# A pool at the far end of SBUF for the expert combination's factors and residuals, and an earlier overflow condition

## The chip, the cores and the metric

The kernel runs on one core of a Trainium2 chip. A core has five engines with a queue of instructions each: TensorE (PE in the profile; PEld is its loading of weights), VectorE (DVE), ScalarE (ACT), GpSimd (POOL) and SyncE (SP), which here mostly starts transfers; sixteen DMA engines carry them. The metric is the device time of one execution in microseconds, 4062.14 us before the change (median of three runs, 4050.82 to 4066.87).

## The reference, cut to what matters

Two blocks of a transformer run one behind the other over 2048 tokens of width 1024. The first ends in a mixture of experts with two experts for a token; the second begins with a norm and one wide projection:

```
# end of the first block
y = hierarchical_moe(h, ...)             # sum over the token's 2 experts: weight * expert's row
x = x + ga2 * rmsnorm(y, ln2_post)       # factor row: ga2 * ln2_post
# begin of the second block
h = rms_norm(x, gain2)
proj = h @ w_in_2                        # split into the inputs of two kinds of attention
```

The experts are a gate, an up and a down product of 1024 x 256, `silu(gate) * up` between them. All products are made in single precision as sums over high and low halves of the operands.

## The kernel before

**Who sets the order.** The program is written out once, in Python. Coroutines (lanes) yield until a model clock (`Clock`, line 35) thinks their operands ready; `B.run` then takes the next, and the order in which operations are written down is each engine's order. A change of what is ready when, or of where a transfer stands, can thus move the order of everything that is planned behind it. Each operation is issued by one helper, so nearly all rows of the profile show line 122, and the tile's name tells which operation it is.

**The experts** (`MoE`, line 1514). Tokens are sorted into 48 tiles of 128 rows: 32 experts and `NBIG` = 16 further tiles for experts with over 128 tokens. A tile's rows are gathered by an indirect DMA of GpSimd (`xg`) and transposed (`xh`). An expert's weights come as six loads of 512 KB (`ld`, four of gate and up, `in_w_gu`, two of down, `in_w_dn`). Each is split into a high half (`whi`, ScalarE) and a low half (`wlo`, VectorE). Then follow the two products (`pA`, and `pU` into `ym`), and a store of `ym` to the tile's rows of `Y` in HBM. The loop of `run` (from line 1656) starts with each tile's first product and ends with the product down of the tile before.

**The overflow** (`Overflow`, line 1689). If an expert had more tokens than its tiles take, a general program would do the whole layer again. Seven small VectorE operations on the counts (`ovm`, `ovj`, `ovn`) make a number `ovi` behind the last tile. `values_load` (line 1710) has every engine load it into a register, and each branches on it at line 1711. With these inputs the general program is skipped.

**The combination** (`Combine`, line 1807) is a lane of the second block's first stage, `S3.run`. `setup` loads the factor row `crow`, spread to all partitions; a load of `gain`, the second block's gain, follows. For each of sixteen blocks of 128 tokens, `block` gathers the two expert rows (`cy0`, `cy1` in the text of the code; the trace calls all of them `cy`) by indirect DMA and loads the residual `cx`. `finish` scales the first (ScalarE), adds the second (VectorE), squares for the norm (ScalarE), multiplies by norm and `crow` (VectorE), adds the residual (GpSimd), stores `X2`, and hands `cx` to the norm of the second block, which squares it again (`jk`), multiplies by `gain` (VectorE) and gives it to TensorE for transposing.

**The weights of the projection** (`Weights`, line 398) have one load buffer here (`b.nld = 1`), and are split like the experts': `whi` on ScalarE, `wlo` on VectorE; the third to sixth go to spare tiles of the combination's pool, `whix` and `wlox`. A load waits for the split of the one before. Eight of the sixteen blocks pass at the start of the stage, the others some 190 us later.

**Pools.** A pool takes its place in SBUF when it is opened and gives it back when it is closed. The combination's pool (`s_c`, in `S3.run`) is opened behind the condition. `crow`, `gain` and `cx` lie in it, so their loads stand behind the branch in SP's queue.

Of the kernel before, what the change touches and what calls it, by code (L numbers as in the profile page):

```python
# [22 lines left out]
T = 2048  # L23
# [184 lines left out]
class B:  # L208
# [15 lines left out]
        nc.vector.memset(self.eps, EPS)  # L224

    @contextmanager
    def pool(self, name):
        with self.tc.tile_pool(name=name, bufs=2, reuse_waits="tile") as p:
            yield Pool(p, self.clock)

    def phase(self, name):
# [1282 lines left out]
class MoE:  # L1514

    def __init__(self, b, H2, Y):
        self.b, self.nc, self.I, self.H2, self.Y = b, b.nc, b.I, H2, Y

        self.at = [t // 3 * 2 + t % 3 // 2 for t in range(NE + NBIG)]
        self.NT = len(self.at)
# [121 lines left out]
    def run(self):  # L1644
        st, en = self.b.phase("mo")
        with st:
            self.setup(en)
            W, NT = self.W, self.NT
            for t in range(4):
                self.gather(t)  # L1650
            W.split(3)
            for _ in self.xT(self.xg[0]):
                pass
            prev = None
            for t in range(NT + 1):
                cur = None
                if t < NT:
                    cur = (self.x, self.at[t])
                    g = self.gu(*cur)
                    next(g), next(g)  # L1660
                if prev:
                    a = self.aT(prev[0])

                W.split(5 + 4 * t + 2)
                if cur:
                    for _ in g:
                        pass
                    s = self.act(self.g)
                xt = self.xT(self.xg[(t + 1) % 4]) if t + 1 < NT else iter(())
                dn = self.down(a, *prev[1:]) if prev else iter(())  # L1670
                for i in range(2):
                    next(dn, None)
                    next(xt, None)
                    if i:
                        next(dn, None)
                for _ in xt:
                    pass
                W.split(5 + 4 * t + 4)
                if t == 2:
                    self.positions()  # L1680
                if t < NT:
                    self.gather(t + 4)
                    prev = (s, cur[1], t)
# [5 lines left out]
class Overflow:  # L1689


    def __init__(self, b, H2, Y, X2, big=NBIG):
        self.b, self.nc, self.I, self.H2, self.Y, self.X2, self.big = b, b.nc, b.I, H2, Y, X2, big

    def run(self):
        b, nc, tc = self.b, self.nc, self.b.tc
        st, en = b.phase("ov")
        with st:

            mx = b.small([128, 1], "ovm")  # L1700
            mi = b.small([128, 1], "ovi", I32)
            nc.vector.tensor_reduce(mx, b.cnt, axis=AX.X, op=OP.max)

            nb, jk = b.small([128, 1], "ovn"), b.small([128, NE], "ovj")
            nc.vector.tensor_scalar(jk, b.cnt, 128.0, None, op0=OP.is_gt, op1=OP.add, accum_out=nb)
            nc.vector.tensor_scalar(nb, nb, float(self.big), None, op0=OP.subtract)
            nc.vector.scalar_tensor_tensor(mx, mx, 256.0, nb, op0=OP.subtract, op1=OP.max)
            nc.vector.tensor_scalar(mx, mx, 0.0, None, op0=OP.max)
            nc.vector.tensor_copy(mi, mx)
            v = nc.values_load(mi[0:1, 0:1], min_val=0, max_val=T)  # L1710
            with tc.If(v > 0):
                with self.b.pool("ov_p") as P:
                    self.general(P)

    def general(self, P):
        b, nc, tc, I = self.b, self.nc, self.b.tc, self.I
# [90 lines left out]
class Combine:  # L1807


    def __init__(self, b, Y, X1, X2, ROW):  # L1810
        self.b, self.nc, self.Y, self.X1, self.X2, self.ROW = b, b.nc, Y, X1, X2, ROW
        self.started = False

    def setup(self, P):
        self.P = P
        self.row = P.tile([128, D], F32, name="crow", bufs=1)
        self.nc.sync.dma_start(self.row, bass.AP(tensor=self.ROW.tensor, offset=self.ROW.offset + 3 * D, ap=[[0, 128], [1, D]]))

    def block(self, blk, then=None):

        b, nc, P = self.b, self.nc, self.P
        ys = []
        for k in range(2):
            y = yield from P.get([128, D], F32, f"cy{k}", bufs=3)
            yield from b.G("indirect_dma_start", out=y, out_offset=None, in_=self.Y,
                           in_offset=bass.IndirectOffsetOnAxis(ap=b.pos[:, k, blk:blk + 1].bitcast(U32), axis=0),
                           bounds_check=self.Y.shape[0] - 1, oob_is_err=False)
            ys.append(y)
        x = yield from P.get([128, D], F32, "cx", bufs=4)
        yield from b.load(x, self.X1[blk * 128:blk * 128 + 128, :])  # L1830
        b.spawn(self.finish(blk, x, *ys, then))

    def finish(self, blk, x, y1, y2, then):
# [24 lines left out]
class S3:  # L1858
# [982 lines left out]
    def run(self):  # L2841
        b, tc, nc, I = self.b, self.b.tc, self.nc, self.I
        unit = [I["w2n"][g, i].rearrange("p k n -> p (k n)") for g in range(6) for i in range(2)]
        unit += [I["w2t"][j].rearrange("p k n -> p (k n)") for j in range(32)]
        unit += self.tail_units()

        order = []
        for u in range(44):
            order.append(u)
            if u - 20 in self.with_tail:  # L2850
                order.append(44 + self.with_tail.index(u - 20))
        self.at = {(0, u): n for n, u in enumerate(order)}
        self.at.update({(1, u): len(order) + u for u in range(44)})
        srcs = [unit[u] for u in order] + list(range(44))
        self.iw = b.const.tile([128, NTB, 8], F32, name="iw")
        self.bad = b.const.tile([128, NTB], F32, name="bad")
        nc.vector.memset(self.bad, 0.0)
        st0, en0 = b.phase("s")
        st0.__enter__()
        with self.b.pool("s_k") as c:  # L2860
            self.consts(c)
            self.keys(c)
            with ExitStack() as st:
                en = lambda name: st.enter_context(b.pool(name))
                b.nld = 1
                self.XN, Wp, self.st = en("s_xn"), en("s_w"), en("s_st")

                with b.pool("s_ro") as c:
                    self.W = Weights(b, c, Wp, srcs, ring=3, ahead=1, store=self.parts, keep=dict(enumerate(order)))
                    b.lanes = [self.weight_lane()]  # L2870
                    self.rope = c.tile([128, NTB, 24], F32, name="rope")
                    with b.pool("s_c") as self.C:
                        if self.comb:
                            self.comb.setup(self.C)
                        self.gain = self.C.tile([128, D], F32, name="gain", bufs=1)
                        nc.sync.dma_start(self.gain, bass.AP(tensor=I["gain2"].tensor, offset=I["gain2"].offset, ap=[[0, 128], [1, D]]))
                        self.W.extra, self.W.hi_eng = (self.C, range(3, 6)), "scalar"
                        b.run(self.norm_lane(), self.proj(0, range(8), groups=True), self.const_lane(), first=b.lanes)
                    fill = chain(self.proj(0, range(8, 32), last=True), self.xn_load(2), self.xn_load(3), self.proj(1, range(12), groups=True))
                    self.W.hi_eng = "gpsimd"  # L2880

                    self.chunked(0, fill, range(2, 8))
                    self.sparse(range(SPLIT), fill)
                    self.go(fill)
                fill = chain(self.keep(), self.proj(1, range(12, 32), last=True))
                self.chunked(1, fill, range(SPLIT, SPLIT + 3))
                self.go(fill)
            with ExitStack() as st:
# [173 lines left out]
def build(tc, I, O):  # L3062
    nc = tc.nc
    with ExitStack() as ctx:
# [9 lines left out]
        with b.pool("keep") as b.keep:  # L3074
            with b.pool("mid") as b.mid:
                with b.pool("big") as H, b.pool("wt") as Wp:
                    p2 = P2(b, mixT, X1, H2, ROW, Wp)
                    P1(b, mixT, H, Wp, p2).run()
                    p2.run()
                MoE(b, H2, Y[2 * T:]).run()  # L3080
                Overflow(b, H2, Y, X2).run()
            S3(b, X2, O["out"], Combine(b, Y, X1, X2, ROW)).run()


# [13 lines left out]
```

## Time and profile before

| | before |
|---|---|
| runs shown | 4050.82, 4062.14, 4066.87 us |
| profiled execution, its own time | 4061.26 us |
| its span in the trace | 4059.4 us |
| mean granted TensorE clock | 0.951 |
| busy: PE, DVE, ACT, POOL | 3646.1, 2734.8, 2283.2, 901.4 us |

A row of a timeline gives the start in microseconds from the span's begin, the duration, the engine, the line, the operation with output tile <- input tiles and shapes, how many of the kind stand in a row, and in brackets how long the engine had idled before and what seems to have ended that. A `q` behind an engine's name is its sequencer, which handles branches, registers and semaphores. The span of a row with several instructions goes from the first's start to the last's end. The releaser is inferred: it is the event that came last by the profile.

### The profile page before, as it was taken

How to read it: one execution, taken by the hardware profiler on the slowest of the kernel's cores; microseconds unless marked ns; L12 is line 12 of the kernel's file. 1: busy time of each engine (PE TensorE's matmuls, PEld its weight loads, DVE VectorE, ACT ScalarE, POOL GpSimd, SP SyncE). 2: the span in 40 equal slices, each digit the busy share in tenths (PEclk: the TensorE clock that was granted, in tenths of full speed). 3: DMA queues.
4: the chain of work that ended last, by engine and by line, in shares of the span. 5: the costliest groups of instructions: out<-in, count | busy, mean ns of one | idle time of the engine just before them, and what ended most of it. 6: DMA issues, size and time to landing. Idle time of an engine off the chain costs nothing.

```text
span 4059.4 us, 64576 instructions
## 1 busy us (share of the span) xinstructions
PE 3646.1 (90%) x21649; PEld 3167.4 (78%) x21649; DVE 2734.8 (67%) x7027; ACT 2283.2 (56%) x4628; POOL 901.4 (22%) x1650
## 2 busy tenths in 40 slices
PE   3999999979969999397999989999889988999997
PEld 2888788768858888296777779888678877999997
DVE  7866785697777777526366743467766656878772
ACT  3654655565546666424257755357667774676751
POOL 1310000031011100473044526111033321211110
PEclk9999999979989999598999989999889998999999
DMA  6233451125358887739887773543166527787767
GB/s 229 79 108 110 137 198 60 64 81 167 130 202 314 314 315 285 263 126 339 290 255 249 249 283 108 169 147 101 43 187 180 173 81 270 259 281 272 265 230 283
DMA packets 425744, 801.28 MB, mean 197 GB/s; under 512 B 129360, under 2 KB 245296, under 8 KB 424496
## 3 DMA queue, kind: packets, MB, share of 16 engines
q1 hardware_dynamic: 407472, 748.70, 54.3%
q0 software_dynamic: 17920, 48.26, 3.5%
q8 instruction: 176, 2.88, 0.3%
q14 instruction: 176, 1.44, 0.1%
HBM read 571.02 MB, written 234.18 MB: 198 GB/s over the span
## 4 chain that ended last, share of the span: by engine, by line
PE 37%; DMA 7%; POOL 4%; DVE 3%; issue 3%; ACT 2%; SPq 1%; POOLq 0%; DVEq 0%; ACTq 0%
PE pA L122 22%; PE pS L122 5%; PE pT L122 5%; PE pU L122 5%; POOL rot L122 1%; DMA x<-IQ 1%; SPq L122 1%; DMA x<-QB 1%; DMA tz<-TZ 1%; POOL st L122 1%; DMA Q<-QA 0%; DMA sg<-SG 0%; DVE scb L122 0%; DVE pp L122 0%; POOL QB L122 0%
## 5 line engine op out<-in xcount | busy, mean ns | idle before, releaser
L122 PE MATMUL pA<-xnl,whi 128*128 128x512 f32 x1024 | 415.3, 406 | 5.4 <-DVE st L122 5.4
L122 DVE TENSOR_TENSOR wlo<-ld,whi 128x1024 fp32r<-128x1024 f32 x271 | 328.7, 1243 | 112.6 <-ACT whi L122 74.8
L122 PE MATMUL pA<-xnh,wlo 128*128 128x512 f32 x1024 | 403.7, 394 | 0.4 <-DVE wlo L122 0.4
L122 PE MATMUL pA<-xnh,whi 128*128 128x512 f32 x1024 | 403.9, 394 | 0.0
L122 DVE TENSOR_TENSOR pp<-pT,pp 128x256 fp32r<-128x256 f32 (+1 forms) x568 | 295.1, 537 | 117.5 <-ACT pp L122 113.8
L122 ACT ACTIVATE pp<-pT 128x256 fp32r<-128x256 f32 (+1 forms) x568 | 260.6, 478 | 201.5 <-PE pT L122 189.3
L122 PE MATMUL pA<-hlo,whi 128*128 128x512 f32 x832 | 352.1, 423 | 10.0 <-issue 6.7
L122 PE MATMUL pA<-hhi,wlo 128*128 128x512 f32 x832 | 328.8, 395 | 0.0
L122 PE MATMUL pA<-hhi,whi 128*128 128x512 f32 x832 | 327.9, 394 | 0.0
L122 ACT ACTIVATE whi<-ld 128x1024 fp32r<-128x1024 f32 x212 | 213.5, 1052 | 59.0 <-PE pA L122 35.3
L122 DVE SCALAR_TENSOR_TENSOR acc<-rl,iw,acc 128x512 f32<-128x512 f32 (+3 forms) x304 | 220.8, 727 | 38.0 <-ACT rl L122 31.4
L122 PEld LDWEIGHTS pA<-xnh,wlo 128*128 128x128 f32 x1024 | 193.9, 189 | 44.8 <-DVE wlo L122 1.1
L122 ACT ACTIVATE bias<-acc,sst 128x1152 f32<-128x1152 f32 (+13 forms) x168 | 220.0, 1309 | 13.3 <-DVE sst L122 9.6
L122 PEld LDWEIGHTS pA<-xnl,whi 128*128 128x128 f32 x1024 | 195.4, 191 | 33.6 <-issue 5.8
L122 PE MATMUL pA<-wlo,xnh 128*128 128x256 f32 (+1 forms) x672 | 200.9, 299 | 22.2 <-DVE st L122 12.4
L122 PEld LDWEIGHTS pA<-xnh,whi 128*128 128x128 f32 x1024 | 194.9, 190 | 29.4
L122 PE MATMUL pU<-pp,vbS 128*128 128x256 f32 x1088 | 203.2, 301 | 10.2 <-DVE pp L122 8.3
L122 ACT ACTIVATE rl<-pS 128x512 f32<-128x512 f32 (+3 forms) x304 | 163.6, 544 | 82.4 <-PE pS L122 42.9
L122 PE MATMUL pA<-whi,xnl 128*128 128x256 f32 (+1 forms) x672 | 197.5, 294 | 4.1 <-DMA xnl<-XND 4.1
L122 PE MATMUL pA<-whi,xnh 128*128 128x256 f32 (+1 forms) x672 | 197.6, 294 | 0.0
L122 ACT ACTIVATE st<-pA 128x256 f32<-128x256 f32 (+4 forms) x160 | 73.6, 460 | 202.6 <-PE pA L122 161.5
L122 PEld LDWEIGHTS pA<-hlo,whi 128*128 128x128 f32 x832 | 159.4, 192 | 35.9 <-issue 9.4
(494 smaller groups left out, 11117.2 us busy)
## 6 DMA issues: line engine op xcount, KB each, us to landing
whi<-W2P SPq DMA_DIRECT2D x172, 512.0 KB
wlo<-W2P SPq DMA_DIRECT2D x172, 512.0 KB
ld<-in_w_gu_dram SPq DMA_DIRECT2D x128, 512.0 KB
ld<-in_w_dn_dram SPq DMA_DIRECT2D x64, 512.0 KB
W2P<-whi SPq DMA_DIRECT2D x57, 512.0 KB
W2P<-wlo SPq DMA_DIRECT2D x57, 512.0 KB
Y<-ym SPq DMA_DIRECT2D x48, 512.0 KB
xl<-in_wadaT_dram SPq DMA_DIRECT2D x32, 512.0 KB
```

The lines of the kernel that those rows point to most:

```text
L122: r = real(*a, **k)
```

## The change

There are three parts. The condition's number is made in tile 4 of the experts (`check`, kept as `ovc` in a pool that stays open), and after the last tile it is only loaded and compared. A pool `pre` is opened ahead of the experts on the other side of SBUF. Four tiles ahead of the end of the loop, `prefetch` takes `crow`, `gain` and the residuals of the first four blocks into it; the later residuals come from the same pool.

```diff
     @contextmanager
-    def pool(self, name):
-        with self.tc.tile_pool(name=name, bufs=2, reuse_waits="tile") as p:
+    def pool(self, name, side=None):
+        with self.tc.tile_pool(name=name, bufs=2, side=side, reuse_waits="tile") as p:
             yield Pool(p, self.clock)
...
# MoE.run, in the loop over tiles
                 if t == 2:
                     self.positions()
+                if t == 4:
+                    self.over.check()
+                if t == NT - 4:
+                    self.comb.prefetch()
...
# Overflow
+    def check(self):
+        b, nc = self.b, self.nc
+        mx = b.small([128, 1], "ovm", bufs=1)
...
+        nc.vector.tensor_copy(mi, mx)
+        self.mi = b.keep.tile([128, 1], I32, name="ovc")
+        nc.vector.tensor_copy(self.mi, mi)
+
     def run(self):
...
-            nc.vector.tensor_copy(mi, mx)
-            v = nc.values_load(mi[0:1, 0:1], min_val=0, max_val=T)
-            with tc.If(v > 0):
+        self.v = self.nc.values_load(self.mi[0:1, 0:1], min_val=0, max_val=T)
+        with self.b.tc.If(self.v > 0):
...
# Combine
+    def open(self):
+        self.pre = self.st.enter_context(self.b.pool("pre", "right"))
+
+    def prefetch(self):
+        b, nc = self.b, self.nc
+        self.row = self.pre.tile([128, D], F32, name="crow", bufs=1)
+        nc.sync.dma_start(self.row, bass.AP(tensor=self.ROW.tensor, ...))
+        self.gain = self.pre.tile([128, D], F32, name="gain", bufs=1)
+        nc.sync.dma_start(self.gain, bass.AP(tensor=b.I["gain2"].tensor, ...))
+        for blk in range(4):
+            x = self.xs[blk] = yield_value(self.pre.get([128, D], F32, "cx", bufs=4))
+            nc.sync.dma_start(x, self.X1[blk * 128:blk * 128 + 128, :])
...
     def setup(self, P):
         self.P = P
-        self.row = P.tile([128, D], F32, name="crow", bufs=1)
-        self.nc.sync.dma_start(self.row, ...)
...
-        x = yield from P.get([128, D], F32, "cx", bufs=4)
-        yield from b.load(x, self.X1[blk * 128:blk * 128 + 128, :])
+        x = self.xs.get(blk)
+        if x is None:
+            x = yield from self.pre.get([128, D], F32, "cx", bufs=4)
+            yield from b.load(x, self.X1[blk * 128:blk * 128 + 128, :])
...
# S3.run
-                        self.gain = self.C.tile([128, D], F32, name="gain", bufs=1)
-                        nc.sync.dma_start(self.gain, ...)
+                        self.gain = self.comb.gain
...
+                    self.comb.st.close()
```

The sync engine's queue in the last expert tiles, before: the last gate and up weights, the last down weights, then the stores of the last tiles.

```order
L122 DMA Y<-ym 128x1024 [waits DVE_49,Activation_49]
L122 ISA
L122 DMA ld<-in_w_gu_dram 128x1024 [waits DMAHW2_49]
L122 ISA
L122 DMA ld<-in_w_gu_dram 128x1024 [waits DMAHW3_49]
L122 ISA
L122 DMA ld<-in_w_dn_dram 128x1024 [waits DMAHW5_49,DMAHW4_49,DVE_49]
L122 ISA
L122 DMA ld<-in_w_dn_dram 128x1024 [waits DMAHW6_49,DVE_49]
L122 DMA Y<-ym 128x1024 [waits DVE_49,Activation_49]
```

The same place after:

```order
L122 ISA
L122 DMA ld<-in_w_gu_dram 128x1024 [waits DMAHW3_49]
L122 DMA crow<-ROW 128x1024 [waits DMAHW4_49]
L122 DMA gain<-in_gain_dram 128x1024 [waits DMAHW5_49]
L122 DMA cx_17135<-X 128x1024 [waits DMAHW6_49]
L122 DMA cx_17137<-X 128x1024 [waits DMAHW7_49]
L122 DMA cx_17139<-X 128x1024 [waits DMAHW0_49]
L122 DMA cx_17141<-X 128x1024 [waits DMAHW1_49]
L122 ISA
L122 DMA ld<-in_w_dn_dram 128x1024 [waits DMAHW2_49,DVE_49]
L122 ISA
L122 DMA ld<-in_w_dn_dram 128x1024 [waits DMAHW3_49,DVE_49]
```

The six loads of `prefetch` stand between the last gate and up load and the two last down loads; the waits in brackets are on the queue slots and engines that must be through before an issue.

ScalarE's queue right behind the branch, before (`cy_0` to `cy_2` are the buffers of the first three blocks; `css`, `crs` the sum of squares and the root of the combination's norm, `nss`, `nrs` those of the next norm):

```order
L122 ACTIVATE cy_0_18911<-cy_0_18911,wts 128x1024
L122 ACTIVATE cy_0_18918,css<-cy_0_18911 128x1024
L122 ACT_TABLE_LOAD
L122 ACTIVATE crs<-css,eps 128x1
L122 ACTIVATE cy_1_18924<-cy_1_18924,wts 128x1024
L122 ACTIVATE cy_2_18935<-cy_2_18935,wts 128x1024
L122 ACTIVATE cy_1_18929,css<-cy_1_18924 128x1024
L122 ACTIVATE jk_18979,nss<-cx_18922 128x1024
L122 ACTIVATE crs<-css,eps 128x1
L122 ACTIVATE nrs<-nss,eps 128x1
L122 ACTIVATE cy_2_18940,css<-cy_2_18935 128x1024
L122 ACTIVATE whi_18957<-ld_18955 128x1024
```

The same place after:

```order
L122 ACTIVATE cy_0_18920<-cy_0_18920,wts 128x1024
L122 ACTIVATE cy_0_18927,css<-cy_0_18920 128x1024
L122 ACTIVATE cy_1_18931<-cy_1_18931,wts 128x1024
L122 ACT_TABLE_LOAD
L122 ACTIVATE crs<-css,eps 128x1
L122 ACTIVATE cy_1_18937,css<-cy_1_18931 128x1024
L122 ACTIVATE cy_2_18941<-cy_2_18941,wts 128x1024
L122 ACTIVATE crs<-css,eps 128x1
L122 ACTIVATE whi_18961<-ld_18959 128x1024
L122 ACTIVATE cy_2_18946,css<-cy_2_18941 128x1024
L122 ACTIVATE crs<-css,eps 128x1
L122 ACTIVATE jk_18998,nss<-cx_17135 128x1024
```

The second block's scale moves ahead of the table load, and the first weight's high half (`whi`) moves up by three places, ahead of the third block's square and the first `jk`.

GpSimd's queue from the third block's add on, before (`rot` and `st` belong to the rotation of projected keys, `rope` is its table):

```order
L122 TENSOR_TENSOR cx_18945<-cx_18945,cy_2_18935 128x1024
L122 DMA cy_2_19081<-Y,pos 128x1024
L122 DMA cy_2_19100<-Y,pos 128x1024
L122 TENSOR_TENSOR cx_18994<-cx_18994,cy_0_18969 128x1024
L122 DMA cy_0_19152<-Y,pos 128x1024
L122 DMA cy_0_19177<-Y,pos 128x1024
L122 TENSOR_TENSOR rot<-st_19169,rope 128x8 x4
L122 TENSOR_TENSOR st_19169<-rot 128x8 x2
L122 TENSOR_TENSOR rot<-st_19169,rope 128x4 x4
L122 TENSOR_TENSOR st_19169<-rot 128x4 x2
L122 COPY st_19169<-st_19169 128x128 x2
L122 TENSOR_TENSOR cx_19056<-cx_19056,cy_1_19023 128x1024
```

The same place after, from the second block's add on:

```order
L122 TENSOR_TENSOR cx_17137<-cx_17137,cy_1_18931 128x1024
L122 TENSOR_TENSOR cx_17139<-cx_17139,cy_2_18941 128x1024
L122 DMA cy_1_19021<-Y,pos 128x1024
L122 DMA cy_1_19053<-Y,pos 128x1024
L122 DMA cy_2_19073<-Y,pos 128x1024
L122 DMA cy_2_19083<-Y,pos 128x1024
L122 TENSOR_TENSOR cx_17141<-cx_17141,cy_0_18985 128x1024
L122 DMA cy_0_19163<-Y,pos 128x1024
L122 DMA cy_0_19182<-Y,pos 128x1024
L122 TENSOR_TENSOR cx_19068<-cx_19068,cy_1_19021 128x1024
L122 TENSOR_TENSOR rot<-st_19164,rope 128x8 x4
L122 TENSOR_TENSOR st_19164<-rot 128x8 x2
```

The third add moves ahead of the two gathers that stood before it, four gathers follow it in a row, and the fifth add moves ahead of the rotations.

## Rows read from the trace of the kernel before

**Rows 1.** Windows: stretch, length, busy PE, PEld, DVE, ACT, POOL, TensorE clock, DMA share, GB/s.

```profile
1600.00:1638.00 38.00, 37.52 (x180) 30.28 (x179) 23.63 (x31) 19.46 (x31) 0.00 (x0) 1.00 0.46 169
1638.00:1675.00 37.00, 0.52 (x4) 0.11 (x2) 17.25 (x57) 11.57 (x18) 16.22 (x11) 0.53 0.73 259
1675.00:1700.00 25.00, 11.12 (x48) 9.75 (x48) 23.07 (x45) 15.96 (x31) 18.74 (x21) 0.50 0.92 340
...
1750.00:1775.00 25.00, 25.00 (x218) 25.00 (x218) 3.30 (x12) 5.26 (x21) 17.90 (x80) 1.00 0.08 32
```

**Rows 2.** VectorE's timeline across the condition.

```profile
1638.54 0.69 DVE L122 COPY ym<-pU 128x512 f32<-128x512 f32 x1 [2.68 <-PE pU L122]
...
1645.58 0.07 DVE L122 MEMSET bad<- 128x16 f32 x1 [5.39 <-DVEq L1711]
```

**Rows 3.** Line 1710, VectorE's register load: min/median/max ns, first and last start.

```profile
L1710 DVEq TENSOR_LOAD <-ovi x1: 1090/1090/1090, 1640.2 to 1640.2; - x1
```

**Rows 4.** Line 1711, VectorE's compare and the event behind it.

```profile
L1711 DVEq COMPARE_BRANCH  x1: 72/72/72, 1641.4 to 1641.4; - x1
...
L1711 DVEq EVENT_SEMAPHORE  x1: 21/21/21, 1645.4 to 1645.4; - x1
```

**Rows 5.** GpSimd's timeline: first gather, first add, rotations, fifth add.

```profile
1646.30 0.98 POOL L122 DMA_INDIRECT cy<-Y,pos  x1 [56.77 <-DMA crow<-ROW]
...
1663.45 3.32 POOL L122 TENSOR_TENSOR cx<-cx,cy 128x1024 f32<-128x1024 f32 x1 [9.70 <-DVE cy L122]
...
1693.60 2.71 POOL L122 TENSOR_TENSOR rot<-st,rope 128x8 f32<-128x8 f32 x4
...
1700.46 2.34 POOL L122 TENSOR_TENSOR cx<-cx,cy 128x1024 f32<-128x1024 f32 x1
```

**Rows 6.** DMA view, 1645 to 1666: gathers' count, median us to landing.

```profile
cy<-Y,pos POOLq DMA_INDIRECT x6, 10.7
```

**Rows 7.** SyncE's timeline: down weights, factors, residuals.

```profile
1610.10 1.47 SPq L122 DMA_DIRECT2D ld<-in_w_dn_dram  x2
...
1642.62 0.33 SPq L122 DMA_DIRECT2D crow<-ROW  x1
1643.06 1.13 SPq L122 DMA_DIRECT2D gain<-in_gain_dram  x1
...
1645.75 1.49 SPq L122 DMA_DIRECT2D cx<-X  x3
```

**Rows 8.** DMA view, 1265 to 1275: one gather of the experts.

```profile
xg<-Y,gidx POOLq DMA_INDIRECT x1, 5.1
```

**Rows 9.** DMA view, 1180 to 1600: the experts' gathers.

```profile
xg<-Y,gidx POOLq DMA_INDIRECT x43, 7.4
```

**Rows 10.** ScalarE's timeline: first scale, table, first weight split.

```profile
1654.73 1.15 ACT L122 ACTIVATE cy<-cy,wts 128x1024 f32<-128x1024 f32 x1 [16.99 <-DMA cy<-Y,pos]
...
1659.68 1.28 ACT L122 ACT_TABLE_LOAD   x1
...
1669.27 1.04 ACT L122 ACTIVATE whi<-ld 128x1024 fp32r<-128x1024 f32 x1
```

**Rows 11.** VectorE's timeline: first sum, first and sixth low halves.

```profile
1657.19 1.28 DVE L122 SCALAR_TENSOR_TENSOR cy<-cy,wts,cy 128x1024 f32<-128x1024 f32 x1 [6.44 <-DMA cy<-Y,pos]
...
1670.34 1.23 DVE L122 TENSOR_TENSOR wlo<-ld,whi 128x1024 fp32r<-128x1024 f32 x1
...
1726.63 1.22 DVE L122 TENSOR_TENSOR wlox<-ld,whix 128x1024 fp32r<-128x1024 f32 x1
```

**Rows 12.** ScalarE's timeline in the last expert tiles.

```profile
1620.02 2.00 ACT L122 ACTIVATE whi<-ld 128x1024 fp32r<-128x1024 f32 x2
1622.54 0.39 ACT L122 ACTIVATE si<-pA 128x256 f32<-128x256 f32 x1 [0.52 <-PE pA L122]
```

**Rows 13.** TensorE's waits, 1950 to 2900: total us, times, longest.

```profile
PE pT L122 <- POOL sc L122: 12.7, 7, 4.1
...
PE pS L122 <- DVE ast L122: 0.2, 1, 0.2
```

More of the change, by code (lines that the diff above doesn't have):

```diff
@@ L1514, with __init__ @@
 class MoE:
-    def __init__(self, b, H2, Y):
-        self.b, self.nc, self.I, self.H2, self.Y = b, b.nc, b.I, H2, Y
+    def __init__(self, b, H2, Y, over, comb):
+        self.b, self.nc, self.I, self.H2, self.Y, self.over, self.comb = b, b.nc, b.I, H2, Y, over, comb
         self.at = [t // 3 * 2 + t % 3 // 2 for t in range(NE + NBIG)]
@@ L1693, in __init__ @@
         self.b, self.nc, self.I, self.H2, self.Y, self.X2, self.big = b, b.nc, b.I, H2, Y, X2, big
-    def run(self):
[L1696 to L1708, printed above, removed]
-            nc.vector.tensor_copy(mi, mx)
-            v = nc.values_load(mi[0:1, 0:1], min_val=0, max_val=T)
-            with tc.If(v > 0):
-                with self.b.pool("ov_p") as P:
-                    self.general(P)
+    def check(self):
+        b, nc = self.b, self.nc
+        mx = b.small([128, 1], "ovm", bufs=1)
+        mi = b.small([128, 1], "ovi", I32, bufs=1)
+        nc.vector.tensor_reduce(mx, b.cnt, axis=AX.X, op=OP.max)
+        nb, jk = b.small([128, 1], "ovn", bufs=1), b.small([128, NE], "ovj", bufs=1)
+        nc.vector.tensor_scalar(jk, b.cnt, 128.0, None, op0=OP.is_gt, op1=OP.add, accum_out=nb)
+        nc.vector.tensor_scalar(nb, nb, float(self.big), None, op0=OP.subtract)
+        nc.vector.scalar_tensor_tensor(mx, mx, 256.0, nb, op0=OP.subtract, op1=OP.max)
+        nc.vector.tensor_scalar(mx, mx, 0.0, None, op0=OP.max)
+        nc.vector.tensor_copy(mi, mx)
+        self.mi = b.keep.tile([128, 1], I32, name="ovc")
+        nc.vector.tensor_copy(self.mi, mi)
+    def run(self):
+        self.v = self.nc.values_load(self.mi[0:1, 0:1], min_val=0, max_val=T)
+        with self.b.tc.If(self.v > 0):
+            with self.b.pool("ov_p") as P:
+                self.general(P)
     def general(self, P):
@@ L1812, in __init__ @@
         self.started = False
+        self.xs = {}
+        self.st = ExitStack()
+    def open(self):
[3 more added lines that the diff above has]
+        self.row = self.pre.tile([128, D], F32, name="crow", bufs=1)
+        nc.sync.dma_start(self.row, bass.AP(tensor=self.ROW.tensor, offset=self.ROW.offset + 3 * D, ap=[[0, 128], [1, D]]))
+        self.gain = self.pre.tile([128, D], F32, name="gain", bufs=1)
+        nc.sync.dma_start(self.gain, bass.AP(tensor=b.I["gain2"].tensor, offset=b.I["gain2"].offset, ap=[[0, 128], [1, D]]))
+        for blk in range(4):
+            x = self.xs[blk] = yield_value(self.pre.get([128, D], F32, "cx", bufs=4))
+            nc.sync.dma_start(x, self.X1[blk * 128:blk * 128 + 128, :])
     def setup(self, P):
         self.P = P
-        self.row = P.tile([128, D], F32, name="crow", bufs=1)
-        self.nc.sync.dma_start(self.row, bass.AP(tensor=self.ROW.tensor, offset=self.ROW.offset + 3 * D, ap=[[0, 128], [1, D]]))
     def block(self, blk, then=None):
@@ L2874, in run @@
                             self.comb.setup(self.C)
-                        self.gain = self.C.tile([128, D], F32, name="gain", bufs=1)
-                        nc.sync.dma_start(self.gain, bass.AP(tensor=I["gain2"].tensor, offset=I["gain2"].offset, ap=[[0, 128], [1, D]]))
+                        self.gain = self.comb.gain
                         self.W.extra, self.W.hi_eng = (self.C, range(3, 6)), "scalar"
                         b.run(self.norm_lane(), self.proj(0, range(8), groups=True), self.const_lane(), first=b.lanes)
+                    self.comb.st.close()
                     fill = chain(self.proj(0, range(8, 32), last=True), self.xn_load(2), self.xn_load(3), self.proj(1, range(12), groups=True))
@@ L3079, in build @@
                     p2.run()
-                MoE(b, H2, Y[2 * T:]).run()
-                Overflow(b, H2, Y, X2).run()
-            S3(b, X2, O["out"], Combine(b, Y, X1, X2, ROW)).run()
+                comb, over = Combine(b, Y, X1, X2, ROW), Overflow(b, H2, Y, X2)
+                comb.open()
+                MoE(b, H2, Y[2 * T:], over, comb).run()
+                over.run()
+            S3(b, X2, O["out"], comb).run()
 def kernel(**inputs):
```

## The prediction

> **What bounds the kernel now.** I began with the busy shares of five stretches around the end of the experts, because every edit lies there. TensorE works 37.5 of 38 us in the last stretch of the experts; then it does half a microsecond of work in 37 us, and in the next 25 us it is busy 11 us at half clock, until it is full again at full clock from 1750 on [rows 1]. So neither TensorE nor any other engine bounds this place. What bounds it is a chain of small waits between the last expert tile and the first product of the next norm, and after it the feed of weights and blocks: DMA is busy 0.92 of 1675 to 1700 and VectorE 23 of 25 us there. What is saved in the chain is worth its full length only if the feed follows.
>
> Second view, VectorE's own timeline of the handover: the last expert copy starts at 1638.54 and lasts 0.69, so ends at 1639.23; the next thing it does outside the condition is a memset at 1645.58 [rows 2]. Between them stand the condition's seven small operations, a register load at 1640.2 of 1.09 us [rows 3], the compare at 1641.4, and an event at 1645.4 that comes 4.0 us after the compare with nothing of the program in between [rows 4]. GpSimd's first gather starts at 1646.30, less than a microsecond after that event [rows 5]. The profile puts this wait down to the load of `crow`, but that is the latest event it can see; the gather needs positions, not factors, so I take VectorE's event as the cause.
>
> Third, what follows the gathers. Six go out 1.29 us apart and take 10.7 us in the median to land [rows 6], while three residuals load on the other queue [rows 7]. In the experts, a gather takes 5.1 us in a quiet window and 7.4 in the median of 43 [rows 8, 9]. ScalarE scales the first pair at 1654.73 [rows 10], VectorE sums it at 1657.19 [rows 11], ScalarE loads its table for 1.28 and at 1669.27 makes the first high half of a weight tile [rows 10]; VectorE makes the low half at 1670.34 [rows 11]. One load buffer serves the weights, so each split lets the next load start; the sixth low half is at 1726.63 [rows 11], and the full stretch of TensorE comes behind it.
>
> **The change, part by part.** *The condition made early.* Seven small operations leave VectorE's path between 1639.23 and 1640.2: that is -1.0 us (bounds 0, if the register load waits for another engine's drain, and -1.7, half of what lies between copy and compare beyond the 1.09 load). The load stays, the compare stays, and the 4.0 us behind it stay [rows 4]: nothing in the diff removes the branch. The same operations (nine now) run on VectorE during the experts, where it is busy 23.6 of 38 us [rows 1]; I cost them at nothing, and with the cover gone they would cost about the 1.0 us again.
>
> [...]
>
> *The prefetch.* It takes `crow`, `gain` and three of the four first `cx`, 2.5 MB, out of the queue that the gathers share after the branch, and a fourth `cx` a little later. They were not waited for themselves: the gain of having them early is only in the gathers. I take 5.7 us to the first landing (bounds 5.1 and 7.4 [rows 8, 9]; nearer to the quiet one, since a weight tile and small tables remain). Before, the first scale came 1654.73 - 1646.30 = 8.4 us after the first gather [rows 5, 10], and the first sum 2.46 later, since the second half of the pair landed so much later. Now: 1645.3 + 5.7 = 1651.0, and the second of the pair one gather (1.3) later, 1652.3, against 1657.19: -4.9 (bounds -2.0 and -6.2).
>
> *The order of the first blocks.* ScalarE now scales the second block's first half ahead of the table load (+1.15, the duration of the first scale [rows 10]), and VectorE puts a reading of the second block's square ahead of the first product with the factors. That square starts behind the root and holds the product 0.7 longer, an estimate from a square of the same shape as the scale less what the four small root operations take anyway. So of -4.9 some 1.9 is given back at once, and GpSimd's first add, at 1663.45 before [rows 5], comes at about 1660.5: -3.0. In exchange the first high half moves up: in ScalarE's list it now stands ahead of the third square and the first norm's square. My walk through the list gives its start between 1660.5 and 1662.5 instead of 1669.27, and the low half at about 1663.8 instead of 1670.34: -6.5.
>
> *What of it reaches the end.* The add's -3.0 moves the blocks; the weights' -6.5 moves the six one-buffer splits up to 1726.63. Since TensorE's full stretch begins behind the last of these, I carry -6.5. A second way to the same size: 3.0 MB less to move in stretches that run at 340 GB/s with DMA 0.92 busy [rows 1] is -8.8 if bytes alone set the pace. And if GpSimd alone set it, -3.0. Both are ends of the range for this term. The second eight blocks, from 1838 on, keep their order, so nothing is added there.
>
> *What the prefetch costs in the experts.* Six issues stand on SP ahead of the last two down-weight loads, which left at 1610.10 in 1.47 us. By the rows of the same transfers after the branch they take 0.33 + 1.13 + 4 x 0.50 = 3.5 us of SP [rows 7], and the 3 MB go ahead of them, about 8.8 us at the 340 GB/s above. The two loads then land around 1619 to 1622 (an estimate: 1610.1, 8.8 and 1 MB more at that rate, or less where queues share). ScalarE splits them from 1620.02, and sits idle 0.52 soon after [rows 12]; TensorE uses them only some 15 us later, in the last tile's second product. So: +0.5, bounds 0 and +2.
>
> Sum: -6.5 (which holds the -1.0 and the -4.9 and what is given back) + 0.5 = -6.0. The profiled execution took 4061.26, so 4055.3; the median of the runs shown is 0.9 above it, so 4056. That is 0.15%, and about 0.5%, 20 us, is what a measurement of this kernel can tell from no change.
>
> [...]
>
> **The rivals.**
> (a) *The gain is paid back to what the blocks allow.* The weights come earlier, but GpSimd's adds and gathers set the pace, and only -3.0 is left: 4061.3 - 3.0 + 0.5 + 0.9 = 4059.7. For it: the first five adds come 9.3 us apart in the mean (1663.45 to 1700.46) although each lasts 2.3 to 3.3 [rows 5], so something other than weights holds them. Against it: the first low half is later than the add it waits with in line. Chance 0.20.
> (b) *The denser lists are worth more than the shift.* Before, the fifth add, at 1700.46, stands right behind a run of rotations on GpSimd from 1693.60 [rows 5], with no idle time between; after, it stands ahead of that run, which is up to 7 us, and the third add comes ahead of two gathers. If block five and all behind it gain 7 us twice over (the run, and the one or two waits of TensorE for the transposes behind it, about the 14 us that TensorE is short in 1675 to 1700 [rows 1]), the time is 4056 - 14 = 4042, or 4049 with half of it. Chance 0.22.
> (c) *Slower: GpSimd's score copies in the second stage.* From about 1950 on, the planner writes another order for GpSimd, VectorE, ScalarE and SP, to the end. TensorE waits there already: of sixteen rows, the largest is 12.7 us in seven waits for GpSimd's `sc`, the smallest 0.2, the sum 60 us [rows 13]. `sc` runs behind rotations and stores in GpSimd's list; if the copy lands behind one more rotation run each time (7 us in the block stage [rows 5]) for two to four of the seven waits, that is +14 to +28, less the 6 gained: 4070 to 4084. It decides from +6 on, where the gain is gone. For it: a planned order that moves at all moves for the whole rest. Against it: its rules are unchanged, so better and worse places are about equally likely. Chance 0.16.
> The change may also do nothing it says: if the gathers' 8.4 us were due to the indirect path alone, only -1.0 + 0.5 would be left, 4061.6; I count that within (a).
>
> **How the numbers follow.** My forecast, 4056, has 0.42; its own range is 4051 to 4060 (term ends -8.8 + 0 and -3.0 + 0.5, with the measurement's own drift of a microsecond or two). (a) 0.20, (b) 0.22, (c) 0.16. To hold 8 in 10 the range reaches into (b) below its 4042 and into (c) up to 4073: 4039 to 4073. Faster by over 0.5% is below 4041.8: half of (b), 0.11, and 0.04 from the shift and the later order both falling well: 0.15. Slower by over 0.5% is above 4082.4: a third of (c), 0.05. The rest, 0.80, is within 0.5%.
>
> **What would show it.** The register load begins right behind the last copy and the 4 us behind the compare are still there; the first gather starts about 1645.3, its landing takes under 7.4 us with one load left beside it, and the six gathers' median falls from 10.7 to near 6. ScalarE's list has the second scale ahead of the table load; the first add is at 1660 to 1661 and the first low half at 1662 to 1665. In the experts ScalarE's last two splits start by 1622 and TensorE has no gap over 1 us before 1638. TensorE is full from about 1731 to 1732 on, 6 us earlier than before. I am wrong if the gathers land as late as before (the queue was not what held them), if the first gather still waits for something other than the branch, if TensorE's idle time in 1638 to 1775 falls by less than 3 or more than 10 us, or if it falls by about 6 and the total differs by more than 10: then the order behind 1950 is what decided.

## The result and the profile after

The changed kernel takes 4105.5 us (median of four runs, 4100.81 to 4112.04) against 4059.81 us (four runs, 4050.82 to 4066.87): ratio 1.0115, 95% interval 1.0089 to 1.0140. It is slower by 46 us, where 6 us of gain were forecast. The profiled execution took 4107.48 us.

Up to the second block the change does about what was forecast, with other prices for its parts. VectorE's timeline of the changed kernel across the branch; the columns are those of [rows 2]:

```profile
1642.87 0.69 DVE L122 COPY ym<-pU 128x512 f32<-128x512 f32 x1 [2.69 <-PE pU L122]
1646.52 0.07 DVE L122 MEMSET bad<- 128x16 f32 x1 [2.96 <-DVEq L1718]
...
1655.43 1.28 DVE L122 SCALAR_TENSOR_TENSOR cy<-cy,wts,cy 128x1024 f32<-128x1024 f32 x1 [5.46 <-DMA cy<-Y,pos]
```

From the end of the last copy to the first memset it is 3.0 us now, 6.35 before [rows 2]. Line 1717 of the changed kernel is the register load; line 1718 is the branch:

```profile
L1717 POOLq TENSOR_LOAD <-ovc x1: 492/492/492, 1588.8 to 1588.8; - x1
...
L1717 DVEq TENSOR_LOAD <-ovc x1: 543/543/543, 1642.9 to 1642.9; - x1
```

```profile
L1718 POOLq COMPARE_BRANCH  x1: 53/53/53, 1589.3 to 1589.3; - x1
...
L1718 DVEq COMPARE_BRANCH  x1: 72/72/72, 1643.5 to 1643.5; - x1
...
L1718 DVEq EVENT_SEMAPHORE  x1: 21/21/21, 1646.4 to 1646.4; - x1
```

Before, all five engines waited for one late value and loaded it at the same moment, 1640.2, in 0.85 to 1.09 us, and VectorE's load took 1.09 us [rows 3]. Now each engine loads when its own list is done: GpSimd at 1588.8, TensorE at 1640.3, ScalarE at 1641.5, VectorE at 1642.9, SyncE at 1644.0, in 0.27 to 0.62 us. VectorE's load starts under the last copy and takes 0.54, and what follows its compare takes 2.9 us instead of 4.0 [rows 4]. TensorE's branch did not get shorter (3.83 us before, 3.88 after).

The prefetch costs more than forecast. ScalarE's timeline in the changed kernel's last expert tiles, and SyncE's:

```profile
1624.59 1.06 ACT L122 ACTIVATE whi<-ld 128x1024 fp32r<-128x1024 f32 x1 [4.03 <-DMA ld<-in_w_dn_dram]
1625.84 1.06 ACT L122 ACTIVATE whi<-ld 128x1024 fp32r<-128x1024 f32 x1 [0.19 <-DMA ld<-in_w_dn_dram]
...
1633.36 0.38 ACT L122 ACTIVATE ah<-pS 128x256 fp32r<-128x256 f32 x1 [4.73 <-PE pS L122]
```

```profile
1608.58 1.09 SPq L122 DMA_DIRECT2D ld<-in_w_gu_dram  x2
1609.72 0.47 SPq L122 DMA_DIRECT2D crow<-ROW  x1
...
1610.71 2.44 SPq L122 DMA_DIRECT2D cx<-X  x4
1613.63 1.59 SPq L122 DMA_DIRECT2D ld<-in_w_dn_dram  x2
```

The last two down-weight loads leave 3.5 us later than before [rows 7] and land behind the 3 MB (10.9 us in the median from issue to landing), and ScalarE, whose next rows are their splits, waits 4.03 us. What stands behind them in its list comes later too (`si` at 1626.80, straight behind the second split), so the last copy comes at 1642.87 instead of 1638.54 [rows 2], 3.9 us later if both are counted from the last gate and up loads, which stood here in the kernel before:

```profile
1608.14 1.10 SPq L122 DMA_DIRECT2D ld<-in_w_gu_dram  x2
```

The gathers land in 6.5 us instead of 10.7 [rows 6] and the low halves are early. From the DMA view of 1645 to 1666, GpSimd's timeline and VectorE's of the changed kernel:

```profile
cy<-Y,pos POOLq DMA_INDIRECT x6, 6.5
```

```profile
1647.71 0.99 POOL L122 DMA_INDIRECT cy<-Y,pos  x1 [57.73 <-DVE half_pow L122]
...
1663.05 3.38 POOL L122 TENSOR_TENSOR cx<-cx,cy 128x1024 f32<-128x1024 f32 x1 [7.88 <-DVE cry L122]
```

```profile
1664.13 3.37 DVE L122 TENSOR_TENSOR wlo<-ld,whi 128x1024 fp32r<-128x1024 f32 x1
...
1723.16 1.22 DVE L122 TENSOR_TENSOR wlox<-ld,whix 128x1024 fp32r<-128x1024 f32 x1
```

The add is 0.4 us earlier, the first low half 6.2, the sixth 3.5 [rows 5, 11]. The last block's transposes on TensorE, before and after, start 5.8 us earlier:

```profile
1943.58 0.60 PE L122 MATMUL pT<-ident,cx 128*128 128x128 f32 x4
```

```profile
1937.81 0.60 PE L122 MATMUL pT<-ident,cx 128*128 128x128 f32 x4
```

So at 1950 the changed kernel is ahead by the 6 us of the forecast. At the end it is behind by 46. The whole loss lies behind 1950, in the second block's attention and the stage at its end, where the diff has no line. The first part of both pages, whole program, before and after:

```profile
PE 3646.1 (90%) x21649; PEld 3167.4 (78%) x21649; DVE 2734.8 (67%) x7027; ACT 2283.2 (56%) x4628; POOL 901.4 (22%) x1650
```

```profile
PE 3662.7 (89%) x21649; PEld 3178.6 (77%) x21649; DVE 2727.8 (66%) x7028; ACT 2285.0 (56%) x4628; POOL 894.3 (22%) x1650
```

TensorE does the same 21649 matrix instructions in 16.6 us more (the mean granted clock fell from 0.951 to 0.947), and the other 29 us are idle time. There is no one new wait. TensorE's waits from 1950 on (us in total, times, longest), before and after:

```profile
PE pT L122 <- DMA x<-QB: 30.7, 8, 26.4
...
PE pT L122 <- DMA x<-IQ: 13.1, 17, 2.5
PE pU L122 <- DVE pp L122: 10.1, 19, 1.4
...
PE pS L122 <- DVE bst L122: 5.0, 12, 1.1
```

```profile
PE pT L122 <- DMA x<-QB: 36.4, 12, 27.9
PE pS L122 <- DVE bst L122: 20.4, 20, 8.9
PE pT L122 <- DMA x<-IQ: 19.1, 15, 4.1
PE pU L122 <- DVE pp L122: 16.5, 22, 2.4
```

The wait that my slow rival named, for GpSimd's `sc` [rows 13], did not grow (15.8 before, 14.0 after). The longest of the `bst` waits shows how an order loses time. VectorE and TensorE of the changed kernel around it:

```profile
2862.08 0.69 DVE L122 SCALAR_TENSOR_TENSOR st<-st,pA 128x512 f32<-128x512 f32 x1 [3.29 <-ACT st L122]
...
2862.87 1.41 DVE L122 TENSOR_SCALAR_CACHE_REDUCE bias<-acc,sst 128x1152 f32<-128x1152 f32 x1
...
2867.39 1.42 DVE L122 SCALAR_TENSOR_TENSOR bias<-acc,sst,big 128x1152 f32<-128x1152 f32 x1
...
2869.77 0.68 DVE L122 CUSTOM_DVE_ANT_0 scb<-pS,bias 128x512 f32<-128x512 f32 x1
```

```profile
2870.52 0.69 PE L122 MATMUL pS<-kbS,qd 128*128 128x128 f32 x2 [8.92 <-DVE bst L122]
```

A selection over 1152 columns stands in VectorE's list ahead of the reading of the scores in `pS`, and TensorE has nothing left in its list ahead of the next scores for `pS`: it stands 8.92 us. In the kernel before TensorE has projection products during the same selection and does not wait (VectorE, then TensorE):

```profile
2844.76 1.41 DVE L122 TENSOR_SCALAR_CACHE_REDUCE bias<-acc,sst 128x1152 f32<-128x1152 f32 x1
```

```profile
2847.04 0.39 PE L122 MATMUL pA<-xnh,whi 128*128 128x512 f32 x1
```

### The profile page after: what moved, and what is told of

It reads as the page before. It is cut to its first block, busy times and chain, and to the rows that moved or that the text cites. A ratio compares the mean times of both kernels' runs of the same rounds, so it can differ in the third digit from the quotient of the medians.

```text
span 4105.4 us, 64561 instructions
## 1 busy us (share of the span) xinstructions
PE 3662.7 (89%) x21649; PEld 3178.6 (77%) x21649; DVE 2727.8 (66%) x7028; ACT 2285.0 (56%) x4628; POOL 894.3 (22%) x1650
## 5 line engine op out<-in xcount | busy, mean ns | idle before, releaser
L122 PE MATMUL pS<-kbS,qd 128*128 128x512 f32 (+3 forms) x640 | 180.2, 386 | 17.1 <-DVE bst L122 16.3
```

The source lines that it names most:

```text
L122: r = real(*a, **k)
```

## The experiments

Times are medians. Ratios are against the kernel before, run on the same chip in the same rounds (4061 to 4065 us in the median), with 95% intervals. Where a run is said to have the old order or the changed kernel's, the traces agree: behind 1965 every engine's operations stand in that order, by operation and tile name. Theory P at first: the loss is the order that the planner writes behind 1950. Rival R: it comes from the moved transfers or the new pool.

**Changed operations, old order.** The clock is told of the old operations at their old places (`ghost` costs the plan the same and issues nothing); the moved ones are issued past it.

```diff
+    def ghost(self, f, *a, **k): ...       # Clock.op without the instruction
# prefetch, check
-        b, nc = self.b, self.nc
+        b, nc = self.b, self.nc._nc
# setup, block, S3.run
+        self.nc.sync.ghost("dma_start", self.row, ...)
+            nc.sync.ghost("dma_start", x, src)
```

> All operations of the changed kernel (early condition, prefetch into the pool at the other end), but the planner's clock is given the old kernel's operations at their old places, so every engine's order is the old one except for the six moved loads. Theory P (the loss is the order that the planner writes behind 1950): the 5 to 6 us gained ahead of 1950 stay and nothing is lost, 4053 to 4056, ratio to before 0.9985 to 0.999. Rival R (the loss comes from the moved transfers or from the place of the new pool): as the changed kernel, 4100 or more, ratio 1.009 or more.

Measured 4072.73, ratio 1.0033 (1.0018 to 1.0048). Neither theory: most of the loss went with the order, but a third of it stayed where P had a gain.

**Old operations, changed order.** The reverse: the clock sees `check` and `prefetch`, the program issues what it did before.

> All operations of the old kernel (late condition, loads behind the branch, pool as before), but the planner's clock is given the changed kernel's operations at their new places, so the order is the changed kernel's except for the six loads. P: the loss behind 1950 without the gain ahead of it, 4105 to 4112, ratio 1.011 to 1.013. R: as before, 4057 to 4063, ratio 1.0.

Measured 4093.68, ratio 1.0078 (1.0061 to 1.0094). The order by itself costs 0.78%, some 31 us; R has no place for that. But P had 1.011 or more: 15 us of the loss are not in the order.

**The early condition alone**, loads behind the branch.

> The early condition alone; the loads stay behind the branch. The order is the old one. P and R alike: the register load comes 1.0 us earlier and all behind it too, 4058 to 4060, ratio 0.9995 to 1.0; the 4 us behind the compare stay.

Measured 4078.28, ratio 1.0039 (1.0026 to 1.0052): a miss for both. Slower by 16 us, with the old order, and with the handover 3.3 us shorter in its trace.

**The prefetch alone**, condition behind the last tile.

> The prefetch alone; the condition is made behind the last tile as before. The order is the changed kernel's. P and R alike: as the changed kernel and 1 us more, 4104 to 4108, ratio 1.011; if it is under 1.008 the early condition has a share in the loss.

Measured 4089.03, ratio 1.0060 (1.0043 to 1.0078), under the 1.008 set as the mark: the early condition has a share in the loss. Beside the second run this leaves -0.18% for the prefetch itself, inside the intervals.

What the early condition changes in the second block is not an instruction but a place: `ovc` is a new tile of 4 bytes in the pool that stays open (18144 to 18400 before, to 18404 after), and all pools of the second block start 32 bytes further, the first attention's at 145696 instead of 145664. The kernels with that tile had longer packets in the attention stages (1024 bytes, 2850 to 3300: 71.5 to 72.6 ns in the mean, 62.5 to 63.6 in the runs so far without it). Theory S was that the place slows the transfers; rival T that the earlier times fall badly.

**Nothing but the 4 bytes.**

```diff
+                if t == 4:
+                    pad = self.b.keep.tile([128, 1], I32, name="pad")
+                    self.nc._nc.vector.memset(pad, 0)
```

> The kernel before with nothing but a tile of 4 bytes in the pool that stays open, written once and never read: every later tile lies 32 bytes further, the order is the old one. Theory S (in the kernels with the early condition it is the place of the later tiles that slows the transfers of the second block's stages, 1950 to 3300): 4075 to 4083, ratio 1.004 to 1.005, and the mean of the 1024-byte packets in 2850 to 3300 goes from 64 ns to 72. Rival T (the early condition's loss comes from earlier times that fall badly behind 1950): 4060, ratio 1.000.

Measured 4080.34, ratio 1.0040 (1.0026 to 1.0054). S, by itself as large as the early condition's loss. The hardware queue's line of the DMA view, 2850 to 3300 (packets, MB, share of 16 engines), of the kernel before and of this one:

```profile
q1 hardware_dynamic: 54640, 61.16, 46.4%
```

```profile
q1 hardware_dynamic: 54496, 61.10, 49.4%
```

The same bytes take 3 points more of the engines' time; packets of 1024 bytes went from 63.6 to 73.5 ns in the mean. By the issues in the same view these are the loads of the attention's `Q`, `K` and `V` (20480 packets, 32 loads of 256 KB, 48 of 128 and 24 of 256); their tiles start 32 bytes past a multiple of 256 here and at one in the kernel before.

**The changed kernel with 64 bytes**, and **the early condition alone with 64 bytes**, on the guess that 64 is what counts:

```diff
-        self.mi = b.keep.tile([128, 1], I32, name="ovc")
-        nc.vector.tensor_copy(self.mi, mi)
+        self.mi = b.keep.tile([128, 16], I32, name="ovc")
+        nc.vector.tensor_copy(self.mi[:, 0:1], mi)
```

> The changed kernel with the kept tile of the condition 64 bytes wide instead of 4, so that every later tile lies 64 bytes further than before instead of 32. The order is the changed kernel's. S: the 16 to 22 us of the place go, 4084 to 4089, ratio 1.006, and packets as before. T: 4105, ratio 1.0115.

> The early condition alone with the kept tile 64 bytes wide; old order. S: the handover's gain of 3 to 4 us is seen by itself, 4056 to 4058, ratio 0.999. T: 4077, ratio 1.004.

Measured 4111.03, ratio 1.0113 (1.0094 to 1.0131), and 4073.57, ratio 1.0023 (1.0010 to 1.0036). The guess was wrong: 64 bytes slow the packets too (68.7 and 69.0 ns). **The late prefetch** (`t == NT - 2` instead of `NT - 4`, 64 bytes, old order):

> Early condition with the 64-byte tile, prefetch two tiles later (behind the last down-weight loads instead of ahead of them), the planner's clock given the old operations, so the old order. S, and the down weights' lateness as the prefetch's price: ScalarE's wait of 3.8 to 4.0 us for the last down weights is gone, the experts end at 1638 again, and all gains stand: 4050 to 4054, ratio 0.9975 to 0.9985. If the prefetch costs something else there, 4056 to 4058. T: 4070 or more.

Measured 4070.69, ratio 1.0017 (1.0005 to 1.0030), a time that T had too; the packets are slow here as well (67.5 ns), so this run does not tell S from T.

**The kept value in a pool at the other end**, so that the second block's pools lie exactly where they lay: for the early condition alone, for the changed kernel, and for the late prefetch.

```diff
-        self.mi = b.keep.tile([128, 1], I32, name="ovc")
+        self.mi = self.pre.tile([128, 1], I32, name="ovc")
```

> The early condition alone, its kept value in a tile at the other end of SBUF, so that from the pools open during the experts' end on no tile of the second block lies elsewhere than before; the order is the old one. Theory S, as it now stands (any move of the later tiles from the places they had slows the second block's transfers, 32 and 64 bytes alike): only the handover's gain of 3.3 us is left, 4057 to 4060, ratio 0.999 to 0.9995, and the 1024-byte packets of 2850 to 3300 are back at 64 ns. Rival U (one more instruction or the early branch itself slows them): ratio 1.002 to 1.004.

> The changed kernel with the kept value of the condition in the new pool at the other end instead of the pool that stays open, so the later tiles lie where they lay before. The order is the changed kernel's. S: 16 to 20 us of the loss go, the order's 31 us stay and the prefetch's own balance with them, 4084 to 4090, ratio 1.006. U: 4105 to 4110, ratio 1.011.

> Early condition, prefetch behind the last down-weight loads, the old order, and no tile of the second block moved. S: all gains and no loss, the handover's 3.3 us and 3 to 4 us of faster gathers, 4053 to 4057, ratio 0.998 to 0.9985. U: 4070, ratio 1.002.

Measured 4059.28, ratio 0.9987 (0.9975 to 1.0000); 4086.59, ratio 1.0057 (1.0043 to 1.0071); 4054.34, ratio 0.9980 (0.9969 to 0.9990). All three as S had it, with the packets of the first at 62.9 ns. The second is the changed kernel with one tile elsewhere: half of its loss is gone. The third beats both kernels by all intervals, if only by 0.2%. Its ScalarE and SyncE in the last expert tiles (the helper's line is 130 here):

```profile
1618.56 2.00 ACT L130 ACTIVATE whi<-ld 128x1024 fp32r<-128x1024 f32 x2
1621.06 0.39 ACT L130 ACTIVATE si<-pA 128x256 f32<-128x256 f32 x1 [0.50 <-PE pA L130]
```

```profile
1608.66 1.47 SPq L130 DMA_DIRECT2D ld<-in_w_dn_dram  x2
...
1625.43 0.42 SPq L1846 DMA_DIRECT2D crow<-ROW  x1
```

With the six loads behind the last down weights ScalarE does not wait for these.

**Another order, nothing else.** The kernel before, its clock pushed once behind 1950:

```diff
+                    b.clock.t["dma"] += 1.0
                     self.chunked(0, fill, range(2, 8))
```

> The kernel before, with the planner's clock told, once, at the end of the second block's first stage, that the transfers are 1.0 us later than it thought. No operation, no tile and nothing ahead of 1950 is changed; the order of all engines behind it is another. Theory L (the old order is a good draw among many that the rules can give, and any push draws anew): slower by 10 to 40 us, ratio 1.003 to 1.01. Rival (the loss of the changed order comes from a particular place that the prefetch moves): 4055 to 4066, ratio 0.999 to 1.001.

Measured 4121.83, ratio 1.0145 (1.0128 to 1.0163): a push of one microsecond in the model costs 59 us on the chip, more than the change did and more than the 10 to 40 of L. No pool lies elsewhere in it (packets 66.6 ns). Two further orders, on the fastest kernel (-0.5 and +2.0):

> The fastest kernel so far (early condition, late prefetch, old places) with the planner's clock told at the end of the first stage that the transfers are 0.5 us earlier than it thought: another order behind 1950, nothing else. If the old order is a chosen good draw: slower than that kernel by 10 to 60 us, ratio to before 1.0 to 1.013. If draws spread evenly around the old one: as likely faster, 0.99 to 0.998.

> The same with 2.0 us later: a third order behind 1950. Good draw: ratio to before 1.0 to 1.013; even spread: as likely 0.99 to 0.998.

Measured 4089.47, ratio 1.0077 (1.0052 to 1.0101), and 4077.18, ratio 1.0038 (1.0023 to 1.0053). With the changed kernel's that is four other orders, all slower than the old one, by 0.6% to 1.5%, each against the kernel that it changes (1.0077 and 1.0038 against 0.9980).

**Which places are slow.** The kernel before with tiles of 128, 512 and 256 bytes (`[128, 32]`, `[128, 128]`, `[128, 64]`) in place of the 4:

> The same with 128 bytes. Alignment to 128: ratio 1.000; alignment to 256 or 512, or any move costs: 1.002 to 1.004, packets at 67 to 73 ns.

> The kernel before with a kept tile of 512 bytes, written once and never read: all later tiles lie 512 bytes further. If it is alignment to a power of two up to 512 that the old places happen to have: as before, ratio 1.000 (0.9985 to 1.0015), packets at 64 ns. If any move costs: as with 32 and 64 bytes, 1.002 to 1.004, packets at 69 to 73 ns.

> The kernel before with a kept tile of 256 bytes, written once and never read: all later tiles lie 256 bytes further. 32, 64 and 128 bytes slowed the packets of 1024 bytes from 64 ns to 69 to 73, 512 bytes did not. If places that are whole multiples of 256 count, as the old ones are: 63 to 65 ns and ratio 0.9985 to 1.0015. If the remainder to 512 counts: 67 ns or more and 1.002 to 1.004.

| all later tiles moved by | ratio (interval) | mean 1024-byte packet, 2850 to 3300 |
|---|---|---|
| 0 (before) | 1 | 63.6 ns |
| 32 | 1.0040 (1.0026 to 1.0054) | 73.5 ns |
| 128 | 1.0032 (1.0021 to 1.0042) | 68.6 ns |
| 256 | 1.0005 (0.9994 to 1.0016) | 63.9 ns |
| 512 | 1.0010 (0.9996 to 1.0024) | 63.7 ns |

In the kernel before, the tiles of `Q`, `K` and `V` start at multiples of 256 (their pool at 145664, 569 times 256). The moves by 256 and 512 leave the packets as they are (63.9 and 63.7 ns), the moves by 32, 64 and 128 slow them (73.5 ns, 68.7 and 69.0 in the kernels above, 68.6).

This is shown for these packets of 1024 bytes only. The buffers of the experts' weight loads lie 224 bytes past a multiple in the kernel before, and the move by 32 puts them on one: the hardware queue's packets of 4096 bytes in 1200 to 1600, most of them these loads, took 173.9 ns in the mean in both kernels.

## Why the prediction was wrong

The step that failed is the one from 1950 to the end. The forecast carried its -6.0 through unchanged; it took a changed order behind 1950 to be as likely better as worse, and put the new tile's place at nothing. The runs showed +0.78% (some 31 us) for the order and +0.40% (some 16 us) for the place.

- *The condition made early*, -1.0 with bounds to -1.7: the direction was right, the size 3.3 us. What was wrong is "the 4.0 us behind it stay": they became 2.9, the load went from 1.09 to 0.54, and it starts 0.7 us ahead of the last copy's end. I had treated the branch as a fixed price; in the kernel before it was five engines loading and branching at one moment. That this crowding is the cause was not tried by itself, and TensorE's branch speaks against it (3.83 and 3.88 us). The bound of -1.7 does not follow from its own words: half of what is left between copy and compare is 0.5, so -1.5 with the -1.0.
- *The gathers*: landing under 7.4 us, median near 6 forecast, 6.5 measured. The first pair's sum followed the first gather by 7.7 us instead of 10.9; 7.0 was forecast. Right, and the prefetch is the cause: the first gathers behind the branch took 10.0 to 11.7 us in the median in the runs with the loads behind it (10.7 before, 10.2 and 11.7 with the early condition alone, 10.0 with the old operations in the changed order) and 6.2 to 6.6 in those with the prefetch (6.5, 6.2 with the prefetch alone, 6.6 in the old order, 6.4 with the late prefetch). That the first gather waits for the branch and not for `crow` was right too: with the prefetch alone, where no load of `crow` follows the branch, it starts 7.7 us after the last copy's start, and 7.8 in the kernel before.
- *The prefetch's cost in the experts*, +0.5 with bounds to +2: it was 3.9. I had the loads landing at 1619 to 1622 from the bytes alone and let TensorE's late use of them cover the rest. The issues on SyncE are 3.5 us late and the bytes come on top, so ScalarE's first split began at 1624.59; and ScalarE's list holds the tile's other work behind it. The cover should have been read from the engine that waits first, not from the last user.
- *The weights' -6.5 and the sum at 1950*: the first low half came 6.2 earlier, the last block 5.8. The sum of -6.0 comes out there by luck: two of its terms were wrong by +3.4 and -2.3, and the sixth low half, on which it was carried, gained only 3.5.
- *The order behind 1950*: this is the ground of rival (c), and not its mechanism. I gave it 0.16 by the sentence "its rules are unchanged, so better and worse places are about equally likely", and at most 28 us for one mechanism. Four other orders were all slower, by 24 to 59 us; if better and worse were equally likely, four of four would be one chance in sixteen. So the old order looks like a good one among many; whether it was looked for, no run here can tell, but in this kernel a reordered rest is a loss until shown otherwise. The mechanism I named, GpSimd's `sc`, was not it: the loss is many small waits of TensorE, for VectorE's `bst` and `pp` and for loads, and a lower granted clock (0.947 against 0.951). With the old program in the changed order `bst` (19.7 us) and `pp` (16.0) are as long, so these belong to the order. The prediction's last sign came (TensorE's idle time in 1638 to 1775 fell by 8.5 us, of which some 4 are expert products that moved into the window, and the total was off by far more than 10), but the order is only part of what it pointed at.
- *A cost I had at nothing and never listed*: the 4-byte tile. It moves the second block's tiles by 32 bytes, and that alone is 0.40%. In this kernel the two causes (0.78% and 0.40%) less the gains of the condition (0.13%) and the prefetch (0.18%) make 0.87%, with the interval of the whole (0.89% to 1.40%) just above that; single terms are known to about 0.15%. The remainder, some 0.3% or 11 us, stays open. Part of it may be that the place costs more in the changed order (1.0115 with the tile moved, 1.0057 without), but the intervals do not part this 0.58% from the 0.40%.

The table shows where the packets were slow, not why: the moves by 256 and 512 bytes left them at 63.9 and 63.7 ns, those by 32 and 128 took them to 73.5 and 68.6. The price does not grow with the distance: they took 16% longer in the mean than the 63.6 ns before when off by 32 and 8% when off by 128, the smaller move being the dearer, and the experts' packets of 4096 bytes no longer at all (173.9 ns in both kernels). So the place is shown as the cause, and how it slows the packets stays open.

## What to carry to other kernels

Where a planner writes the order, split any change in two by giving the model the old operations with the new program and the reverse: that shows in two runs how much of the loss is the redrawn order. A new tile in a long-lived pool moves all that is allocated behind it; look where the large tiles start, and put the new one at the other end (packets at 62.9 ns here) or try larger pads: here 256 and 512 bytes left the packets at 63.9 and 63.7 ns, and 64 and 128 bytes did not (67.5 to 69.0). Read a transfer's new cost from the first engine that waits for it.

## What the runs showed of the hardware

In the kernel before and its copies with nothing but a tile added, loads of rows of 1024 bytes into SBUF took 63.6 to 63.9 ns a packet in the mean with the tiles of `Q`, `K` and `V` at multiples of 256 bytes (moves by 0, 256 and 512) and 68.6 to 73.5 ns off them (128 and 32), with the order unchanged; packets of 4096 bytes of the experts' stage took 173.9 ns with their buffers 224 bytes past a multiple and at one. A register load on VectorE took 1.09 us when five engines loaded at the same moment, 1640.2, and 0.54 us when no other engine's load lay beside it, and its stretch from compare to event 4.0 and 2.9 us; TensorE's branch took 3.83 and 3.88 us. Six indirect gathers of 512 KB landed in 10.7 us in the median beside the loads of factors and residuals and in 6.5 us with these moved ahead.
